# Differential attention scores from 64-row to 128-row matmuls, in a two-layer encoder

## The chip, the cores and the metric

One core of one Trainium2 chip runs the whole program. The metric is the device time of one execution in microseconds, as the median over the runs of a kernel; lower is better. A profile is taken of one further execution, and its trace tells when each instruction of each engine ran: TensorE (PE, matmuls, with its weight loads as PEld), VectorE (DVE), ScalarE (ACT), GpSimd (POOL), and SyncE (SP), which here only issues the weight transfers.

## What is computed

The reference is a trunk of two layers on 256 tokens of width 2048, all in float32. Cut to what matters here, a layer is:

```python
z = rmsnorm(x, g_mix[i]) @ w_in[i]
dq, dk, dv, cq, ckv, kr, ga, gb = jnp.split(z, split_at, axis=-1)
# differential attention: 8 heads, each with two maps of 64 columns of queries and keys
dq = apply_partial_rope(dq...); dk = apply_partial_rope(dk...)
scores = jnp.einsum('bqhcd,bkhcd->bhcqk', qb, kh) * 64 ** -0.5
probs = jax.nn.softmax(scores, axis=-1)
weights = probs[:, :, 0] - lam * probs[:, :, 1]
A = jnp.einsum('bhqk,bkhe->bqhe', weights, v)
# latent attention B: q from cq @ w_q_up, k and v from ckv @ w_kv_up, 8 heads of 128 + 64 columns
merged = sigmoid(ga) * (rmsnorm(A) @ w_branch_diff) + sigmoid(gb) * (B @ w_branch_mla)
x = x + merged @ w_out
x = x + SwiGLU(rmsnorm(x))
x = x + sigmoid(rmsnorm(x) @ w_ple_gate) * (p @ w_ple_in)
```

Head h of the differential attention has 128 columns of queries and 128 of keys; the first 64 belong to map 0 and the last 64 to map 1. Each map has its own 256x256 scores.

## The kernel before

**Layout.** Activations are held transposed: 128 features on the partitions, 256 tokens along the row. To keep float32 accuracy at the speed of the faster float32r matmul, every operand is kept as two parts: `hi` is the value rounded to float32r (an ACT copy) and `lo` is the rest (a DVE subtraction). An activation operand such as `ua[j]` is one tile of 512 columns, `hi` in the first 256 and `lo` in the last 256.

**Products.** `product` (with `piece` and `emit`) makes one 128x256 output tile: for each 128x128 weight tile one matmul with `hi` of the weight against the 512 columns (L219) and one with `lo` of the weight against the first 256 columns (L223). The weights come in pieces of eight such tiles. A piece costs one transfer on SP's queue into `w`, one ACT copy into `whi` (L194) and one DVE subtraction into `wlo` (L76). `whi` and `wlo` have three buffers each, `w` four. `joined` (L247) adds the two halves of the result: an ACT copy `join` and a DVE addition into a tile `a`.

**Differential head h.** `queries_keys(h)` makes the query product and the key product; each is joined, rotated (DVE: a stream shuffle, two multiplications, an addition, each 256 wide) and split into `hi` and `lo` by `split` (L254). Queries go to `ub[h]`, keys to `fa(h)`. `diff_weights(h)` then makes the scores: `three` (L410) names three pairs, hi x lo, lo x hi and hi x hi, for the rows 0 to 63 (map 0) and the rows 64 to 127 (map 1), and `scores` (L413) issues them for two blocks of 128 queries, the two maps alternating. These are twelve matmuls of 64 rows (L421). Both maps go through `exps` (DVE maximum, scaling, two ACT exponentials, DVE reciprocal) and are combined into `E`. `turned` transposes `E` on PE (L439) and `diff_out` multiplies with the values (L679).

**Order.** A scheduler that orders instructions by a simulated timeline writes the order of every engine's queue; each engine then takes its own queue strictly in order and waits on semaphores. The source gives it the program: `pipelined` walks over the heads, and between the steps of one head the generator `beside` supplies other work: the up-projections of the latent keys (`keys_up`, L604 on), the next head's `queries_keys`, the rotated shared key, and after the last head the latent queries and the first tiles of the gate `ga` (`gate`). Gate tiles 0 to 6 are made early into spare scratch tiles, and the first two of them go to the `sq` scratch buffers.

**Names.** In the trace `S` is a scores bank, `mm` a product bank, `at` a small bank (transposes, attention output), `E` the attention weights, `nm` the negated row maxima. The latent attention's scores come from the same `scores` function, with operands of all 128 rows (`fb` keys, `fa` queries, `kr` the rotated shared key): ten matmuls a head.

Of the kernel before, what the change touches and what calls it, by code (L numbers as in the profile page):

```python
# [12 lines left out]
F32 = mybir.dt.float32  # L13
F32R = mybir.dt.float32r
I32 = mybir.dt.int32
AF = mybir.ActivationFunctionType
ALU = mybir.AluOpType
AX = mybir.AxisListType

P = 128  # L20
T = 256
# [3 lines left out]
DH = 8  # L25
# [29 lines left out]
def encoder(ctx, tc, x, p, positions, cols, lams, wq, wk, wv, wcq, wckv, wkr, wga, wgb,  # L55
            w_q_up, w_kn, w_v, w_bd, w_bm, w_out, w_gate, w_up, w_down, w_pin, w_pg, rope_c, out):
    nc = tc.nc
    V, A, PE = nc.vector, nc.scalar, nc.tensor
# [4 lines left out]
    tmp = pool("tmp")  # L63
    stat = pool("stat")
# [4 lines left out]
    def scratch(tag, bufs, n=T):  # L69
        return tmp.tile([P, n], F32, tag=tag, name=tag, bufs=bufs)  # L70
# [4 lines left out]
    def tt(o, a, b, op):  # L75
        return V.tensor_tensor(out=o, in0=a, in1=b, op=op)  # L76

    def stt(o, a, s, b, op0, op1):
        return V.scalar_tensor_tensor(out=o, in0=a, scalar=s, in1=b, op0=op0, op1=op1)

    def ts(o, a, s1, s2, op0, op1=ALU.bypass):
        return V.tensor_scalar(out=o, in0=a, scalar1=s1, scalar2=s2, op0=op0, op1=op1)  # L82


    ua = [const.tile([P, 2 * T], F32R, name=f"ua{j}") for j in range(NC)]
# [8 lines left out]
    def operand(t):  # L94
        return t.rearrange("p c t -> p (c t)")
# [131 lines left out]
    def product(src, us, inside=None):  # L227


        acc = bank(ps_mm, "mm", "mm")  # L230
        n = len(us)
        for a in range(0, n, PT):
            m = min(PT, n - a)
            hi, lo = piece(src[:, a * P : (a + m) * P], m)
            emit(acc, hi, lo, 0, us[a : a + m], a == 0, a + m == n, inside and (inside[0] - a, inside[1]))
        return acc
# [10 lines left out]
    def joined(acc, o=None):  # L247
        t = scratch("join", 3)
        A.activation(t, acc[:, T:], AF.Copy)  # L249
        o = scratch("a", 4) if o is None else o  # L250
        tt(o, acc[:, :T], t, ALU.add)
        return o

    def split(u, src, gain=None):  # L254
        hi, lo = u[:, :T], u[:, T:]
        if gain is None:
            return A.activation(hi, src, AF.Copy), tt(lo, src, hi.bitcast(F32), ALU.subtract)  # L257
        return A.activation(hi, src, AF.Copy, scale=gain), stt(lo, src, gain, hi.bitcast(F32), ALU.mult, ALU.subtract)
# [108 lines left out]
    for t in krs:  # L367
        nc.gpsimd.memset(t.bitcast(F32), 0.0)

    def rotated(a, c_, s_, o=None):  # L370
        if o is None:
            r = bank()[:, :T]
            PE.matmul(r, halves, a, start=True, stop=True)
        else:
            r = a
        t = scratch("sh", 2)
        V.stream_shuffle(t, r, SWAP16)
        tt(t, t, s_, ALU.mult)
        tt(a, r, c_, ALU.mult)
        tt(a, a, t, ALU.add)  # L380
        if o is None:
            hi, rest = krs
            A.activation(hi[:, :T], a, AF.Copy)
            for j in range(2):
                s, t = slice(64 * j, 64 * j + 64), slice(j * T, (j + 1) * T)
                tt(rest[s, t], a[s], hi[s, :T].bitcast(F32), ALU.subtract)
        else:
            A.activation(o.rearrange("p (h t) -> p h t", h=2), a.rearrange("p (h t) -> p h t", h=1).to_broadcast([P, 2, T]), AF.Copy)
            for j in range(2):
                s, t = slice(64 * j, 64 * j + 64), slice(j * T, (j + 1) * T)  # L390
                tt(o[64 - 64 * j : 128 - 64 * j, t], a[s], o[s, t].bitcast(F32), ALU.subtract)

    def narrow(src, us):

# [15 lines left out]
    def three(q, k):  # L410
        return [(q[:, :T], k[:, T:]), (q[:, T:], k[:, :T]), (q[:, :T], k[:, :T])]

    def scores(*maps):  # L413


        Ss = [bank(ps_s, "S", "S", (P, 2, T)) for _ in maps]
        for b in range(2):
            for j in range(len(maps[0])):
                for S, pairs in reversed(list(zip(Ss, maps))):
                    q, k = pairs[j]  # L420
                    PE.matmul(S[:, b, :], q[:, b * P : (b + 1) * P], k, start=j == 0, stop=j == len(pairs) - 1)  # L421
        return Ss

    def exps(S, E, scale):

        nm, sm, rs = (stat.tile([P, 2], F32, tag=t, name=t, bufs=4) for t in ("nm", "sm", "rsum"))
        V.tensor_reduce(out=nm, in_=S, axis=AX.X, op=ALU.max, negate=True)
        ts(nm, nm, scale, None, ALU.mult)
        for b in range(2):
            last_exp[0] = A.activation(E[:, b, :], S[:, b, :], AF.Exp, bias=nm[:, b : b + 1], scale=scale, accum_out=sm[:, b : b + 1])  # L430
        V.reciprocal(out=rs, in_=sm)
        return rs
# [72 lines left out]
    for L in range(DEPTH):  # L505
# [40 lines left out]
            tt(o, t, R, ALU.mult)  # L546


        qk = [(ub[h], operand(fa(h, F32R))) for h in range(DH)]

        def queries_keys(h, *inside):
            for which, w in enumerate((wq, wk)):
                a = joined(product(w[L, h], ua, inside=(8, inside[which]) if inside else None))
                sh = scratch("sh", 2)
                V.stream_shuffle(sh, a, ROPE16)
                tt(sh, sh, sr, ALU.mult)
                tt(a, a, cr, ALU.mult)
                tt(a, a, sh, ALU.add)
                split(qk[h][which], a)


        cq, ckv = ub[8:12], ub[12:14]
# [41 lines left out]
        def beside():  # L604

            for h in range(2, DH):
                if h < 6:
                    keys_up(2 * h - 4)
                elif h == 7:
                    rotated(joined(narrow(wkr[L], ua)), crm, srm)  # L610
                yield
                queries_keys(h)
                yield
            for n in (8, 0, 2, 10):
                if n == 0:
                    settle(0)
                gate(wga, gate_a, next(todo))
                queries_up(n)
                yield
            settle(4)  # L620
            for n in (4, 6):
                gate(wga, gate_a, next(todo))
                queries_up(n)
            gate(wga, gate_a, next(todo))

        def gate(w, store, n):
            tt(store(n), joined(product(w[L, n], ua)), R, ALU.mult)
# [34 lines left out]
        def diff_weights(h):  # L662
            q, k = qk[h]
            E = [weights(), weights("E1")]
            halves = [slice(c * 64, (c + 1) * 64) for c in range(2)]
            r = [exps(S, e, 0.125) for S, e in zip(scores(*(three(q[d], k[d]) for d in halves)), E)]
            ts(r[1], r[1], neg_lam[:, L : L + 1], None, ALU.mult)
            for b in range(2):
                A.activation(E[0][:, b, :], E[0][:, b, :], AF.Copy, scale=r[0][:, b : b + 1])
                stt(E[0][:, b, :], E[1][:, b, :], r[1][:, b : b + 1], E[0][:, b, :], ALU.mult, ALU.add)  # L670
            return E[0]

        def diff_out(h, W):
# [347 lines left out]
```

## Time and profile before

| | |
|---|---|
| median of 3 runs | 2827.76 us (2827.31 to 2827.99) |
| profiled execution, its own time | 2827.12 us |
| its span, first to last instruction | 2825.3 us |
| granted TensorE clock | 0.999 |
| PE busy, PEld busy | 100%, 88% |
| DVE busy, ACT busy | 74%, 54% |
| transfers | 531 MB, mean 188 GB/s |

The differential heads run from about 106 to 211 us of the span in layer 0 and from about 1510 to 1615 us in layer 1. In the timelines the first column is the start, the second the duration. A matmul's duration there is its whole passage through the array; matmuls overlap, so what one costs is read from the distance of one start to the next.

### The profile page before, as it was taken

To read this page: it belongs to the slowest core of one execution; us is meant where nothing else is said; L and a number is where in the kernel's file an instruction comes from. 1 tells how busy PE (TensorE), PEld (TensorE's weight loads), DVE (VectorE), ACT (ScalarE), POOL (GpSimd) and SP (SyncE) were. 2 spreads that over 40 slices of the span, in tenths; PEclk is the share of its full clock that TensorE was granted. 3 is DMA by queue.
4 is the path that set the end of the run, shared out by engine and by line. 5 is a ranking of instruction groups with operands and counts; after the bars stand their busy time and mean duration, and the time that the engine had idled before them with its cause. 6 is when DMAs were issued, how large, how long until landed. Compare 5 with 4: busy or idle time off the path is not lost.

```text
span 2825.3 us, 43994 instructions
## 1 busy us (share of the span) xinstructions
PE 2816.8 (100%) x16691; PEld 2490.3 (88%) x16691; DVE 2080.3 (74%) x3573; ACT 1534.1 (54%) x2556; POOL 1.9 (0%) x15
## 2 busy tenths in 40 slices
PE   9999999999999999999999999999999999999998
PEld 8888988888888888888888889888888888888888
DVE  8998668776666666677869976687766666666777
ACT  7676546554444444455646765465544444444556
POOL 0000000000000000000000000000000000000000
PEclk9999999999999999999999999999999999999999
DMA  7545456555665566666665454555566655655654
GB/s 246 174 162 172 157 186 197 193 193 194 188 198 194 190 194 198 193 194 193 194 193 166 157 173 157 193 198 193 194 194 189 198 193 185 202 194 194 193 193 155
DMA packets 158325, 531.37 MB, mean 188 GB/s; under 512 B 17184, under 2 KB 25376, under 8 KB 158112
## 3 DMA queue, kind: packets, MB, share of 16 engines
q1 hardware_dynamic: 157680, 527.96, 58.2%
q8 instruction: 131, 2.15, 0.3%
q14 instruction: 82, 0.67, 0.1%
q10 hardware_dynamic: 432, 0.59, 0.1%
HBM read 526.39 MB, written 2.10 MB: 187 GB/s over the span
## 4 chain that ended last, share of the span: by engine, by line
PE 99%; DMA 0%; DVE 0%; SPq 0%; DVEq 0%; ACT 0%; issue 0%
PE mm L219 61%; PE mm L223 31%; PE S L421 1%; PE mmv L481 1%; PE mmv L483 1%; PE mmv L482 1%; PE at L439 1%; PE at L679 1%; PE at L735 0%; PE mm L826 0%; PE mm L407 0%; DMA w<-in_wv 0%; PE at L694 0%; PE at L332 0%; PE mm L882 0%; PE at L300 0%
## 5 line engine op out<-in xcount | busy, mean ns | idle before, releaser
L194 ACT ACTIVATE whi<-w 128x1024 fp32r<-128x1024 f32 (+2 forms) x1038 | 1065.9, 1028 | 1224.9 <-issue 593.4
L76 DVE TENSOR_TENSOR wlo<-w,whi 128x1024 fp32r<-128x1024 f32 (+2 forms) x1038 | 1225.8, 1182 | 648.0 <-ACT whi L194 642.3
L219 PE MATMUL mm<-ub,whi 128*128 128x512 f32 x3936 | 1340.5, 389 | 0.0
L219 PE MATMUL mm<-ua,whi 128*128 128x512 f32 x3712 | 1274.0, 390 | 0.0
L223 PE MATMUL mm<-ub,wlo 128*128 128x256 f32 x3936 | 1084.6, 276 | 0.0
L223 PE MATMUL mm<-ua,wlo 128*128 128x256 f32 x3712 | 1027.4, 277 | 0.0
L219 PEld LDWEIGHTS mm<-ub,whi 128*128 128x128 f32 x3936 | 737.8, 188 | 151.8
L219 PEld LDWEIGHTS mm<-ua,whi 128*128 128x128 f32 x3712 | 696.2, 188 | 141.5
L223 PEld LDWEIGHTS mm<-ub,wlo 128*128 128x128 f32 x3936 | 738.8, 188 | 1.3
L223 PEld LDWEIGHTS mm<-ua,wlo 128*128 128x128 f32 x3712 | 697.1, 188 | 2.0
L76 DVE TENSOR_TENSOR a<-mm,join 128x256 f32<-128x256 f32 (+1 forms) x423 | 174.8, 417 | 1.7 <-ACT join L855 1.4
L249 ACT ACTIVATE join<-mm 128x256 f32<-128x256 f32 x452 | 165.6, 368 | 6.3 <-PE mm L223 5.7
L76 DVE TENSOR_TENSOR xT<-xT,mm 128x256 f32<-128x256 f32 x256 | 106.9, 420 | 40.8 <-PE mm L223 37.0
L76 DVE TENSOR_TENSOR a<-a,row 128x256 f32<-128x256 f32 (+1 forms) x209 | 87.6, 422 | 5.9
L76 DVE TENSOR_TENSOR a<-a 128x256 f32<-128x256 f32 x120 | 50.9, 425 | 4.0
L76 DVE TENSOR_TENSOR ua<-a,ua 128x256 fp32r<-128x256 f32 x120 | 50.0, 418 | 1.0 <-ACT ua L257 1.0
L257 ACT ACTIVATE ua<-a 128x256 fp32r<-128x256 f32 x120 | 48.1, 403 | 2.6 <-DVE a L76 2.6
L481 PE MATMUL mmv<-whi,ua 128*128 128x512 f32 x128 | 49.0, 394 | 0.4 <-ACT whi L194 0.2
L430 ACT ACTIVATE E<-S,nm 128x256 f32<-128x256 f32 x96 | 44.2, 472 | 8.0 <-DVE nm L82 8.0
L482 PE MATMUL mmv<-whi,ua 128*128 128x512 f32 x128 | 48.4, 391 | 0.0
L483 PE MATMUL mmv<-wlo,ua 128*128 128x512 f32 x128 | 42.4, 392 | 0.0
L76 DVE TENSOR_TENSOR ssq<-ssq,sq 128x256 f32<-128x256 f32 x96 | 40.2, 419 | 0.3 <-ACT sq L287 0.3
(207 smaller groups left out, 1211.4 us busy)
## 6 DMA issues: line engine op xcount, KB each, us to landing
w<-in_w_gate SPq DMA_DIRECT2D x176, 512.0 KB, 4.6
w<-in_w_up SPq DMA_DIRECT2D x176, 512.0 KB, 4.7
w<-in_w_down SPq DMA_DIRECT2D x128, 512.0 KB, 4.2
w<-in_wga SPq DMA_DIRECT2D x64, 512.0 KB, 3.8
w<-in_wgb SPq DMA_DIRECT2D x64, 512.0 KB, 3.8
w<-in_w_out SPq DMA_DIRECT2D x64, 512.0 KB, 4.6
w<-in_w_pg SPq DMA_DIRECT2D x64, 512.0 KB, 4.6
w<-in_w_down SPq DMA_DIRECT2D x64, 384.0 KB, 3.7
```

The source lines that it names most:

```text
L76: return V.tensor_tensor(out=o, in0=a, in1=b, op=op)
L194: last_split[:] = A.activation(hi[:, s], w[:, s], AF.Copy), tt(lo[:, s], w[:, s], hi[:, s].bitcast(F32), ALU.subtract)
L219: lead = PE.matmul(acc, hi[:, s], u, start=start, stop=False)
L223: rest = PE.matmul(acc[:, T:], lo[:, s], u[:, :T], start=False, stop=stop)
L249: A.activation(t, acc[:, T:], AF.Copy)
L257: return A.activation(hi, src, AF.Copy), tt(lo, src, hi.bitcast(F32), ALU.subtract)
L421: PE.matmul(S[:, b, :], q[:, b * P : (b + 1) * P], k, start=j == 0, stop=j == len(pairs) - 1)
L430: last_exp[0] = A.activation(E[:, b, :], S[:, b, :], AF.Exp, bias=nm[:, b : b + 1], scale=scale, accum_out=sm[:, b : b + 1])
L439: PE.transpose(tp[:, kb, b * P : (b + 1) * P], W[:, b, kb * P : (kb + 1) * P], ident)
L481: PE.matmul(banks[k][b], xh, hi[:, s], start=c == 0, stop=False)
L482: PE.matmul(banks[k][b], xl, hi[:, s], start=False, stop=False)
L483: last_mm[:] = [PE.matmul(banks[k][b], xh, lo[:, s], start=False, stop=c == n - 1)]
```

## The change

The scores of a differential head are made with all 128 rows. The tile that `stacked` writes has, for map 0, the `hi` of the queries in rows 0 to 63 and their `lo` in rows 64 to 127 (first 256 columns), and for map 1 the `lo` in rows 0 to 63 and the `hi` in rows 64 to 127 (last 256 columns). The key tile of each map holds the same 64 rows of keys twice, in both row halves: a `split` on 64 rows and then an ACT copy of the 64x512 result to the other half. One matmul against the keys' `lo` and one against their `hi` then give all products of a map, so a head has two maps x two matmuls x two query blocks = eight matmuls in place of twelve. The product lo x lo, which was left out before, is now in the sum.

With it the two products of a head are joined into one tile of 2 x 256 columns (`qk`, taken from the tag `wt`), so that the shuffle and the three rotation steps run once at 512 wide instead of twice at 256. The key tiles alternate between `fa(4), fa(5)` and `fa(6), fa(7)`. In `diff_weights` the two maps' maxima, sums and reciprocals lie in one tile of four columns, which saves one scaling and one reciprocal a head. Last, in `beside` one gate tile is made before the first `keys_up`, and the one that stood at the end is gone; the number of gate tiles is the same.

```diff
--- before.py
+++ after.py
@@ -367,6 +367,12 @@
     for t in krs:
         nc.gpsimd.memset(t.bitcast(F32), 0.0)
 
+    def stacked(o, a):
+        A.activation(o.rearrange("p (h t) -> p h t", h=2), a.rearrange("p (h t) -> p h t", h=1).to_broadcast([P, 2, T]), AF.Copy)
+        for j in range(2):
+            s, t = slice(64 * j, 64 * j + 64), slice(j * T, (j + 1) * T)
+            tt(o[64 - 64 * j : 128 - 64 * j, t], a[s], o[s, t].bitcast(F32), ALU.subtract)
+
     def rotated(a, c_, s_, o=None):
         if o is None:
             r = bank()[:, :T]
@@ -385,10 +391,7 @@
                 s, t = slice(64 * j, 64 * j + 64), slice(j * T, (j + 1) * T)
                 tt(rest[s, t], a[s], hi[s, :T].bitcast(F32), ALU.subtract)
         else:
-            A.activation(o.rearrange("p (h t) -> p h t", h=2), a.rearrange("p (h t) -> p h t", h=1).to_broadcast([P, 2, T]), AF.Copy)
-            for j in range(2):
-                s, t = slice(64 * j, 64 * j + 64), slice(j * T, (j + 1) * T)
-                tt(o[64 - 64 * j : 128 - 64 * j, t], a[s], o[s, t].bitcast(F32), ALU.subtract)
+            stacked(o, a)
 
     def narrow(src, us):
 
@@ -546,17 +549,27 @@
             tt(o, t, R, ALU.mult)
 
 
-        qk = [(ub[h], operand(fa(h, F32R))) for h in range(DH)]
+        qk = {}
+
+        def two(row):
+            return row.rearrange("p (h t) -> p h t", h=1).to_broadcast([P, 2, T])
 
         def queries_keys(h, *inside):
+            a, sh = (tmp.tile([P, 2, T], F32, tag="wt", name=n, bufs=4) for n in ("qk", "qksh"))
             for which, w in enumerate((wq, wk)):
-                a = joined(product(w[L, h], ua, inside=(8, inside[which]) if inside else None))
-                sh = scratch("sh", 2)
-                V.stream_shuffle(sh, a, ROPE16)
-                tt(sh, sh, sr, ALU.mult)
-                tt(a, a, cr, ALU.mult)
-                tt(a, a, sh, ALU.add)
-                split(qk[h][which], a)
+                joined(product(w[L, h], ua, inside=(8, inside[which]) if inside else None), a[:, which, :])
+            V.stream_shuffle(operand(sh), operand(a), ROPE16)
+            tt(sh, sh, two(sr), ALU.mult)
+            tt(a, a, two(cr), ALU.mult)
+            tt(a, a, sh, ALU.add)
+            q, k = a[:, 0, :], a[:, 1, :]
+            ks = [operand(fa(j + (4 if h in (1, 3, 5) else 6), F32R)) for j in range(2)]
+            qk[h] = ub[h], ks
+            stacked(ub[h], q)
+            for j in range(2):
+                s, t = slice(64 * j, 64 * j + 64), slice(64 - 64 * j, 128 - 64 * j)
+                split(ks[j][s], k[s])
+                A.activation(ks[j][t], ks[j][s].bitcast(F32), AF.Copy)
 
 
         cq, ckv = ub[8:12], ub[12:14]
@@ -604,6 +617,8 @@
         def beside():
 
             for h in range(2, DH):
+                if h == 2:
+                    gate(wga, gate_a, next(todo))
                 if h < 6:
                     keys_up(2 * h - 4)
                 elif h == 7:
@@ -621,7 +636,6 @@
             for n in (4, 6):
                 gate(wga, gate_a, next(todo))
                 queries_up(n)
-            gate(wga, gate_a, next(todo))
 
         def gate(w, store, n):
             tt(store(n), joined(product(w[L, n], ua)), R, ALU.mult)
@@ -662,12 +676,21 @@
         def diff_weights(h):
             q, k = qk[h]
             E = [weights(), weights("E1")]
-            halves = [slice(c * 64, (c + 1) * 64) for c in range(2)]
-            r = [exps(S, e, 0.125) for S, e in zip(scores(*(three(q[d], k[d]) for d in halves)), E)]
-            ts(r[1], r[1], neg_lam[:, L : L + 1], None, ALU.mult)
+            qs = [q[:, d * T : (d + 1) * T] for d in range(2)]
+            Ss = scores(*([(a, b[:, T:]), (a, b[:, :T])] for a, b in zip(qs, k)))
+            nm, sm, r = (stat.tile([P, 4], F32, tag=t, name=t, bufs=2) for t in ("nm4", "sm4", "r4"))
+            for d, S in enumerate(Ss):
+                V.tensor_reduce(out=nm[:, 2 * d : 2 * d + 2], in_=S, axis=AX.X, op=ALU.max, negate=True)
+            ts(nm, nm, 0.125, None, ALU.mult)
+            for d, S in enumerate(Ss):
+                for b in range(2):
+                    j = 2 * d + b
+                    last_exp[0] = A.activation(E[d][:, b, :], S[:, b, :], AF.Exp, bias=nm[:, j : j + 1], scale=0.125, accum_out=sm[:, j : j + 1])
+            V.reciprocal(out=r, in_=sm)
+            ts(r[:, 2:], r[:, 2:], neg_lam[:, L : L + 1], None, ALU.mult)
             for b in range(2):
-                A.activation(E[0][:, b, :], E[0][:, b, :], AF.Copy, scale=r[0][:, b : b + 1])
-                stt(E[0][:, b, :], E[1][:, b, :], r[1][:, b : b + 1], E[0][:, b, :], ALU.mult, ALU.add)
+                A.activation(E[0][:, b, :], E[0][:, b, :], AF.Copy, scale=r[:, b : b + 1])
+                stt(E[0][:, b, :], E[1][:, b, :], r[:, 2 + b : 3 + b], E[0][:, b, :], ALU.mult, ALU.add)
             return E[0]
 
         def diff_out(h, W):
```

Three places show how the order moved. The first is PE's queue around the scores of head 1, first before, then changed (`S` is the scores bank, `fa` the keys, `ub` the queries, `at<-ident,E` the transposes).

```order
L219 MATMUL mm<-ua_84,whi 128x512
L421 MATMUL S<-fa_640,ub_93 128x256 x12
L439 MATMUL at<-ident,E 128x128 x4
L223 MATMUL mm<-ua_84,wlo 128x256
L219 MATMUL mm<-ua_85,whi 128x512
```

```order
L223 MATMUL mm<-ub_105,wlo 128x256
L442 MATMUL at<-ident,E 128x128 x4
L424 MATMUL S<-fa_1236,ub_93 128x256
L424 MATMUL S<-fa_1235,ub_93 128x256
...
L219 MATMUL mm<-ua_76,whi 128x512
L223 MATMUL mm<-ua_76,wlo 128x256
```

The run of twelve has become eight that alternate between the two key tiles (two of them are shown), they stand behind the transposes instead of ahead of them, and they stand between two products instead of inside one.

The second place is ACT's queue where the keys of head 1 become ready (before: `fa_640` are its keys, `a` its rotated product; changed: `ub_93` its queries, `fa_1235` and `fa_1236` its two key tiles).

```order
L194 ACTIVATE whi<-w_1560 128x1024
L669 ACTIVATE E<-E,rsum 128x256 x2
L257 ACTIVATE fa_640<-a 128x256
L194 ACTIVATE whi<-w_1582 128x1024
L249 ACTIVATE join<-mm 128x256 x2
```

```order
L371 ACTIVATE ub_93<-qk 128x512
L257 ACTIVATE fa_1235<-qk 64x256
L257 ACTIVATE fa_1236<-qk 64x256
L194 ACTIVATE whi<-w_1513 128x512
L249 ACTIVATE join<-mm 128x256
L257 ACTIVATE fb_1349<-a 128x256
L692 ACTIVATE E<-E,r_1261 128x256 x2
L194 ACTIVATE whi<-w_1581 128x1024
L572 ACTIVATE fa_1235<-fa_1235 64x512
L572 ACTIVATE fa_1236<-fa_1236 64x512
L194 ACTIVATE whi<-w_1603 128x1024
```

One ACT step on the keys has become four (two on 64 rows by 256, two on 64 rows by 512), and the queries' step has become one of 512 columns; they stand between the weight splits `whi` in the same queue.

The third is SP's queue of weight transfers in layer 0, behind the key weights of head 1.

```order
L191 DMA w_1180<-in_wk 128x1024
L191 DMA w_1202<-in_wk 128x1024
L191 DMA w_1290<-in_w_kn 128x2x256
L191 DMA w_1365<-in_wq 128x1024
L191 DMA w_1387<-in_wq 128x1024
```

```order
L191 DMA w_1167<-in_wk 128x1024
L191 DMA w_1189<-in_wk 128x1024
L191 DMA w_1277<-in_wga 128x1024
L191 DMA w_1299<-in_wga 128x1024
L191 DMA w_1326<-in_w_kn 128x2x256
L191 DMA w_1394<-in_wq 128x1024
```

The two transfers of the early gate tile have moved ahead of the first latent-key weights, and everything behind them comes two transfers later.

## The prediction, made before the change was run

> **What bounds the kernel now.** I read the page first, its busy line and its chain of waits.
>
> ```profile
> PE 2816.8 (100%) x16691; PEld 2490.3 (88%) x16691; DVE 2080.3 (74%) x3573; ACT 1534.1 (54%) x2556; POOL 1.9 (0%) x15
> PE 99%; DMA 0%; DVE 0%; SPq 0%; DVEq 0%; ACT 0%; issue 0%
> ```
>
> TensorE works without a break, and 99% of the chain that ends last is PE. So two things alone can move the time: what a matmul costs on PE, and a new wait that stops PE. No wait is there to be removed. A busy PE hides its own inefficiency, though, so I went on to the timeline of PE. Around the scores of head 1 it reads:
>
> ```profile
> 123.31 0.39 PE L219 MATMUL mm<-ua,whi 128*128 128x512 f32 x1
> 123.54 0.28 PE L223 MATMUL mm<-ua,wlo 128*128 128x256 f32 x1
> 123.65 0.39 PE L219 MATMUL mm<-ua,whi 128*128 128x512 f32 x1
> 123.88 0.28 PE L223 MATMUL mm<-ua,wlo 128*128 128x256 f32 x1
> 123.99 0.39 PE L219 MATMUL mm<-ua,whi 128*128 128x512 f32 x1
> 124.31 0.98 PE L421 MATMUL S<-fa,ub 64*128 64x256 f32 x12
> 125.22 0.66 PE L439 MATMUL at<-ident,E 128*128 128x128 f32 x4
> 125.63 0.36 PE L223 MATMUL mm<-ua,wlo 128*128 128x256 f32 x1
> 125.83 0.40 PE L219 MATMUL mm<-ua,whi 128*128 128x512 f32 x1
> 126.06 0.28 PE L223 MATMUL mm<-ua,wlo 128*128 128x256 f32 x1
> 126.18 0.39 PE L219 MATMUL mm<-ua,whi 128*128 128x512 f32 x1
> ```
>
> From start to start an undisturbed L219 matmul costs 0.23 us (123.31 to 123.54) and an L223 matmul 0.11 us. The twelve scores take 0.91 us from their first start to the next work (124.31 to 125.22). That is 0.076 us each, less than an undisturbed matmul of the same 256 columns, so two 64-row matmuls run side by side. But the L219 matmul ahead of them takes 0.32 us instead of 0.23: PE loses 0.09 us on entering the block. At head 0, where products follow directly, the edges show on both sides:
>
> ```profile
> 106.48 0.28 PE L223 MATMUL mm<-ub,wlo 128*128 128x256 f32 x1
> 106.68 0.97 PE L421 MATMUL S<-fa,ub 64*128 64x256 f32 x12
> 107.58 0.50 PE L219 MATMUL mm<-ub,whi 128*128 128x512 f32 x1
> 107.92 0.28 PE L223 MATMUL mm<-ub,wlo 128*128 128x256 f32 x1
> ```
>
> Entering costs 0.20 - 0.11 = 0.09 us, the twelve 0.90 us, and the first matmul behind them 0.34 instead of 0.23 us, 0.11 more. A block of half-row scores thus takes 1.10 us of PE. Scores with all 128 rows are in the trace too, in the latent attention:
>
> ```profile
> 309.52 0.28 PE L223 MATMUL mm<-ua,wlo 128*128 128x256 f32 x1
> 309.64 0.52 PE L421 MATMUL S<-fb,fa 128*128 128x256 f32 x3
> 310.00 0.40 PE L421 MATMUL S<-kr,fc 128*128 128x256 f32 x2
> 310.24 0.52 PE L421 MATMUL S<-fb,fa 128*128 128x256 f32 x3
> 310.60 0.40 PE L421 MATMUL S<-kr,fc 128*128 128x256 f32 x2
> 310.83 0.60 PE L439 MATMUL at<-ident,E 128*128 128x128 f32 x4
> 311.19 0.48 PE L219 MATMUL mm<-ua,whi 128*128 128x512 f32 x1
> 311.50 0.28 PE L223 MATMUL mm<-ua,wlo 128*128 128x256 f32 x1
> ```
>
> Ten of them take 1.19 us (309.64 to 310.83), 0.119 us each, and the matmul ahead of them takes 0.12 us, 0.01 more than undisturbed. The four transposes take 0.36 us and leave the next product 0.08 us late (0.31 for 0.23). In the block of head 1 transposes follow as well and take 0.41 us with the product behind them 0.09 us late (0.20 for 0.11), so there only 0.05 us of that belongs to the half-row scores: its block costs 0.09 + 0.91 + 0.05 = 1.05 us.
>
> **The change on PE.** Removed: twelve half-row matmuls a head, 1.05 to 1.10 us; I take 1.08. Added: eight full-row matmuls, 8 x 0.119 = 0.95 us, plus 0.01 at the entry, 0.96. What a product directly behind a full-row block loses is not in these rows: nothing at best, the 0.11 us of head 0 at worst. I take nothing, since the entry shows none and the whole array is in use on both sides. So a head gains 0.12 us, and 16 heads (8 in each of two layers) gain 1.9 us. Bounds: at worst 1.05 - 0.96 - 0.11 = -0.02 us a head, a loss of 0.3 us in all; at best 1.10 - 8 x 0.11 = 0.22 us (full-row matmuls as fast as an undisturbed L223), 3.5 us in all. The gate tile moves 16 pairs of matmuls, 16 x 0.34 = 5.4 us of PE, and its two transfers from one place to another, and adds none.
>
> **The change on DVE and ACT.** They are off the chain, so their terms are nothing as long as PE has its operands in time. How far from the limit they are is shown by the stretch of the differential heads (columns of the last row: PE, PEld, DVE and ACT busy, with counts) and by the groups in it:
>
> ```profile
> core 0: us, PE busy (x) PEld busy (x) DVE busy (x) ACT busy (x) POOL busy (x), PEclk, DMA share, GB/s
> 111.50:222.90 111.40, 111.40 (x718) 97.67 (x717) 106.26 (x270) 84.55 (x215) 0.00 (x0) 1.00 0.49 160
> L76 DVE TENSOR_TENSOR a<-mm,join 128x256 f32<-128x256 f32 x34 | 13.8, 417 | 0.1
> L76 DVE TENSOR_TENSOR fa<-a,fa 128x256 fp32r<-128x256 f32 x11 | 4.6, 421 | 0.2 <-ACT fa L257 0.2
> L76 DVE TENSOR_TENSOR wlo<-w,whi 128x512 fp32r<-128x512 f32 x3 | 2.0, 682 | 0.0
> L555 DVE STREAM_SHUFFLE sh<-a 128x256 f32<-128x256 f32 x13 | 5.8, 445 | 0.0
> L76 DVE TENSOR_TENSOR ub<-a,ub 64x256 fp32r<-64x256 f32 x4 | 1.7, 420 | 0.1
> L431 DVE RECIPROCAL rsum<-sm 128x2 f32<-128x2 f32 x16 | 2.5, 158 | 0.5 <-ACT E L430 0.2
> L82 DVE TENSOR_SCALAR nm<-nm 128x2 f32<-128x2 f32 x16 | 2.1, 160 | 0.0
> L249 ACT ACTIVATE join<-mm 128x256 f32<-128x256 f32 x34 | 12.5, 377 | 1.4 <-PE mm L223 1.1
> L194 ACT ACTIVATE whi<-w 128x1024 fp32r<-128x1024 f32 x38 | 40.4, 1064 | 21.0 <-PE mm L219 17.8 <-issue 1.4 <-ACT join L249 1.0
> L257 ACT ACTIVATE fa<-a 128x256 fp32r<-128x256 f32 x11 | 4.6, 422 | 0.9 <-DVE a L76 0.9
> L388 ACT ACTIVATE ub<-a 128x512 fp32r<-128x512 f32 x2 | 1.3, 644 | 0.0
> ```
>
> DVE, a head: the two shuffles and six rotation steps (2 x 0.445 + 6 x 0.42 = 3.41 us) become four steps of 512 columns. A shuffle of 512 is not in the trace; I price it like the 512-wide subtraction, 0.68 (below by one 256-wide shuffle, 0.445, above by two, 0.89), so 4 x 0.68 = 2.72. Two subtractions become four on 64 rows, which cost no less than on 128 (0.420 against 0.421): +0.84. One scaling and one reciprocal go: -0.32. The sum is -0.17 us a head (-0.41 to +0.04): DVE stays at its 95%. ACT, a head: two splits of 0.42 become one of 512 columns (0.64), two on 64 rows (0.42 each) and two copies of 64x512 (0.64 each, on the same grounds): 2.76 for 0.84, +1.9 us. Some seven heads in the stretch add 13 us to ACT's 84.55 of 111.4, and it has 26.9 us idle there. So there is room, but ACT's idle time falls by half, and the added steps stand in the same queue as the `whi` splits, each waiting for DVE: behind them wait the next `whi`, then DVE's `wlo`, then PE.
>
> The longer way from the key product to the scores is the second danger. Before: join 0.38, addition 0.42, shuffle 0.445, three steps 1.26, split 0.42 and 0.42, 3.3 us. After: 0.38 + 0.42 + four steps of 0.68 + the queries' split 0.64 + key split 0.42 and 0.42 + two copies 1.28 = 6.3 us, 3.0 more. The smallest margin that I found before is at head 7, where the last key operand is written here and the scores start there:
>
> ```profile
> 203.09 0.42 DVE L76 TENSOR_TENSOR fa<-a,fa 128x256 fp32r<-128x256 f32 x1
> 206.69 0.97 PE L421 MATMUL S<-fa,ub 64*128 64x256 f32 x12
> ```
>
> 206.69 - 203.51 = 3.2 us, just over the 3.0. The new order also puts more PE work between a head's key product and its scores: counted out in both orders at 0.34 us a pair, 10.3 us became 22.2 at head 7 and 12.1 became 14.7 at head 0; only head 2 loses (18.3 to 16.3), head 3 keeps 16. So I cost the waits at nothing. The gate tile is part of this: 5.4 us of PE work that asks DVE for two `wlo` and two small steps, where the heads ask it for more.
>
> **The sum.** The profiled execution took 2827.12 us, 1.8 us around its span of 2825.3. Less 1.9 it comes to 2825.2. The median of the runs is 0.64 us higher than that execution, so the forecast for the median is 2827.76 - 1.9 = **2825.9 us**, 0.07% faster. I count 0.2%, 5.7 us, as what a measurement of this kernel tells from no change; the forecast lies inside.
>
> **Rivals.** *The edges stay.* Half-row matmuls run in pairs, so twelve need six slots and the change needs eight; if the 0.09 and 0.11 us at the edges come from changing between products and scores, and not from the half rows, they remain. Then a head pays 8 x 0.119 - 0.905 = +0.05 us, 0.8 us in all: 2828.5, not faster, within 0.2%. Against it stands the latent block, whose entry costs 0.01. The Trainium skill's page TensorEngine Tiling (Array Packing), under Overview (Theoretical Speedup) and Tiling Modes (Key Properties), speaks against the change: tiles of half the rows run independently, up to twice as fast; by that alone six slots of 0.119 become eight, 16 x 0.24 = +3.8 us, 2831.6. The same list says that a change of tiling mode drains TensorE; the 0.09 us at the entry and 0.11 behind agree with that, and the 0.90 us for six pairs, 0.15 a pair, is not the full doubling either.
>
> *Scores come late (slower).* If each of the three added ACT steps stands behind one `whi` split of 1.06 us, the way grows by 3.0 + 3.2 = 6.2 us against a margin of 3.2. At the heads whose cover does not grow PE then waits: head 3 3.0 us, head 2 5.0, 8.0 a layer, 16 in all, less 1.9: 2841.9, 0.5% slower. It decides from the point where the way has grown by more than margin and added cover. For it: DVE at 95% and both engines strictly in order. Against it: the 26.9 us that ACT has idle, and a PE order with 14.7 us or more behind every key product.
>
> *Fewer matmuls, plainly.* 64 fewer at the 0.28 us of a row is 18 us: 2809.9, 0.6% faster. Against it: a duration is a passage through the array, and all sixteen old blocks together cost 16 x 1.08 = 17 us.
>
> **Chances.** Forecast 0.77, edges stay 0.12, scores late 0.07, plain count 0.02, something else 0.02. The likeliest is the time I predict. Its own range from the bounds is 2824.3 (all of the 3.5 us) to 2828.1 (a loss of 0.3). The 8 in 10 takes in the edges that stay and small waits, half a microsecond more than those 2828.5: 2829.0; downward I add 0.5 us for pairs that run at 0.35 us behind a half-row block (125.83 to 126.18) instead of 0.34 (123.31 to 123.65): 2823.8. Faster by over 0.2% (under 2822.1) 0.02; slower by over 0.2% (above 2833.4), most of the late scores, 0.05; within 0.93.
>
> **What would show it.** In the profile after, eight scores in 0.95 us with the matmul ahead at its undisturbed distance show the first term; 0.2 us still lost at the edges shows the first rival. A PE that stays in the chain for 99%, with no wait for DVE or ACT at the scores or at L223 around 110 to 215 us, shows the second. ACT's busy time should rise by 16 x 1.9 = 30 us and DVE's fall slightly. The prediction is wrong if PE stands idle for more than 2 us in a layer, or if full-row blocks slow the pairs behind them.

## The result, and the profile after

| | before | after |
|---|---|---|
| median of 9 runs each | 2827.35 us (2826.82 to 2827.99) | 2835.35 us (2834.55 to 2836.84) |
| ratio, 95% interval | | 1.0029 (1.0020 to 1.0038) |
| span of the profiled execution | 2825.3 us | 2833.5 us |

The changed kernel is 8.0 us slower, 0.29%. The forecast was 2825.9 us with a range up to 2829.0: the sign was wrong, and the time lies outside the range. The busy line and the chain of the changed kernel's page, and below them PE's own waits in its trace (total, times, longest):

```profile
PE 2817.6 (99%) x16627; PEld 2496.0 (88%) x16627; DVE 2087.9 (74%) x3493; ACT 1564.1 (55%) x2604; POOL 1.9 (0%) x15
PE 97%; ACT 2%; DVE 0%; issue 0%; DMA 0%; DVEq 0%; SPq 0%; ACTq 0%
PE mm L219 <- DVE qk L76: 5.9, 6, 1.6
PE at L500 <- DVE ones L116: 1.0, 1, 1.0
PE at L717 <- DVE ub L79: 0.8, 2, 0.4
PE mm L219 <- DVE a L76: 0.5, 2, 0.2
PE mmv L484 <- ACT whi L194: 0.4, 1, 0.4
```

PE's own waits in the kernel before were these, and the only one of this size is the 1.0 us for `ones` at the start:

```profile
PE at L497 <- DVE ones L116: 1.0, 1, 1.0
PE mmv L481 <- ACT whi L194: 0.2, 1, 0.2
```

PE now waits 7.2 us more in the heads and behind them, 5.9 of it in six waits for one kind of instruction: the DVE addition that joins a product into `qk`. PE's busy time rose by 0.8 us, although it was to fall by 1.9. So the span's 8.2 us are waits, about 7.4 (with 0.2 more at `mmv`), and 0.8 us of busy time. That is not work that was added: there are 64 matmuls fewer, but the first one behind a wait shows 0.47 us where 0.39 is usual. The stretch of the differential heads in layer 0 shows the same (columns as in the prediction):

```profile
111.50:222.90 111.40, 108.32 (x663) 96.37 (x662) 101.75 (x213) 90.91 (x213) 0.00 (x0) 1.00 0.49 159
```

PE stands for 3.1 of 111.4 us, more than the 2 us a layer that the prediction named as the sign of being wrong, and DVE, the supposed tight engine, is less busy than before (101.75 against 106.26). Nothing is overloaded. Something is out of place.

**Where PE stands.** PE's timeline after the scores of head 1:

```profile
126.63 0.60 PE L442 MATMUL at<-ident,E 128*128 128x128 f32 x4
127.38 1.21 PE L424 MATMUL S<-fa,ub 128*128 128x256 f32 x8
130.15 0.47 PE L219 MATMUL mm<-ua,whi 128*128 128x512 f32 x1 [1.56 <-DVE qk L76]
...
145.73 0.47 PE L219 MATMUL mm<-ua,whi 128*128 128x512 f32 x1 [0.69 <-DVE qk L76]
...
161.22 0.47 PE L219 MATMUL mm<-ua,whi 128*128 128x512 f32 x1 [0.69 <-DVE qk L76]
```

Behind the scores of heads 1, 2 and 3 the first matmul of a query product waits, and the same three waits come again about 1407.6 us later in layer 1. The product does not read `qk`. By the names in the built order it writes a product bank: the product banks (`mm`) are four, given out in turn, and the query product that starts at 130.15 (head 3's) gets the bank of the query product of head 2, which is free only when DVE has added its two halves. When ACT and DVE did that, their timelines tell:

```profile
123.60 0.36 ACT L249 ACTIVATE join<-mm 128x256 f32<-128x256 f32 x1
...
124.97 1.04 ACT L194 ACTIVATE whi<-w 128x1024 fp32r<-128x1024 f32 x1
126.04 1.28 ACT L572 ACTIVATE fa<-fa 64x512 fp32r<-64x512 f32 x2
127.35 1.06 ACT L194 ACTIVATE whi<-w 128x1024 fp32r<-128x1024 f32 x1
```

```profile
128.44 1.22 DVE L76 TENSOR_TENSOR wlo<-w,whi 128x1024 fp32r<-128x1024 f32 x1 [1.17 <-ACT whi L194]
129.58 0.75 DVE L76 TENSOR_TENSOR qk<-mm,join 128x256 f32<-128x256 f32 x2
```

ACT had its half of the query's join ready at 123.96. The addition comes at 129.58, 5.6 us later and side by side with the key's (x2). It is not late because DVE has no time: DVE stands idle for 1.17 us ahead of the step in front of it. It is late because it was written behind that step, a `wlo` split, in DVE's queue, whose `whi` came late because ACT made the two key copies between its splits. The chain of waits in the window from 126 to 131 us names these links (start, length, what):

```profile
126.69 0.63 ACT fa L572
...
127.35 1.07 ACT whi L194
...
128.44 0.58 DVE wlo L76
129.02 0.56 issue
129.58 0.43 DVE qk L76
130.01 0.14 issue
130.15 0.47 PE mm L219
```

**What else the trace shows.** An undisturbed block, at head 4:

```profile
176.38 0.39 PE L219 MATMUL mm<-ua,whi 128*128 128x512 f32 x1
176.61 1.12 PE L424 MATMUL S<-fa,ub 128*128 128x256 f32 x8
177.57 0.28 PE L223 MATMUL mm<-ua,wlo 128*128 128x256 f32 x1
```

Eight scores take 0.96 us, and the matmul ahead keeps its 0.23 us: the first term stands as forecast. By the distances from start to start and their usual values, the blocks of heads 1 to 3 cost 3.18, 1.89 and 1.91 us in place of 0.97, which is 4.1 us of excess a layer; another 0.6 us a layer is lost later, at 232 us, where the transposes of the attention output in `settle` wait 0.4 us and the product behind them 0.2.

### The profile page after: what moved, and what is told of

Read it like the earlier page. It is cut to its first block, busy times and chain, and to the rows that moved or that the text cites. A ratio compares the mean times of both kernels' runs of the same rounds, so it can differ in the third digit from the quotient of the medians.

```text
span 2833.5 us, 43839 instructions
## 1 busy us (share of the span) xinstructions
PE 2817.6 (99%) x16627; PEld 2496.0 (88%) x16627; DVE 2087.9 (74%) x3493; ACT 1564.1 (55%) x2604; POOL 1.9 (0%) x15
## 4 chain that ended last, share of the span: by engine, by line
PE 97%; ACT 2%; DVE 0%; issue 0%; DMA 0%; DVEq 0%; SPq 0%; ACTq 0%
PE mm L219 60%; PE mm L223 30%; PE mmv L486 1%; PE mmv L484 1%; PE mmv L485 1%; PE S L424 1%; ACT whi L194 1%; PE at L702 1%; PE at L758 0%; PE at L442 0%; PE mm L849 0%; ACT E L688 0%; PE mm L410 0%; ACT fa L572 0%; DVE wlo L76 0%
## 5 line engine op out<-in xcount | busy, mean ns | idle before, releaser
L76 DVE TENSOR_TENSOR a<-mm,join 128x256 f32<-128x256 f32 x391 | 161.9, 417 | 1.5 <-ACT join L878 1.4
L76 DVE TENSOR_TENSOR a<-a,sig 128x256 f32<-128x256 f32 x92 | 38.4, 419 | 0.0
```

## The experiments

Three theories were to be told apart. **A, the join's place:** the merged tile `qk` and its shuffled partner take their buffers from the tag `wt` (a tag names a set of buffers, here four, that its tiles share), which also serves the transposed weights, and this holds the query's join back in DVE's queue, so that a product bank comes free late. **B, the load:** the key copies and the longer way to the scores take too much of ACT and DVE, so that operands come late whatever the buffers. **C, the gate tile:** putting it early does harm. All medians stand beside the kernel before on the same chip, which took 2827.2 to 2827.3 us in each comparison.

**1. Own buffers for the merged tile.** From the changed kernel, with four buffers in all as it had, only split by use (the second part of the latent attention's transposed weights moves to the new two as well):

```diff
-        wt = [tmp.tile([P, 2, T], F32R if parts else F32, tag="wt", name="wt", bufs=4) for _ in range(1 + parts)]
+        wt = [tmp.tile([P, 2, T], F32R if parts else F32, tag=("wt", "qs")[j], name="wt", bufs=2) for j in range(1 + parts)]
...
-            a, sh = (tmp.tile([P, 2, T], F32, tag="wt", name=n, bufs=4) for n in ("qk", "qksh"))
+            a, sh = (tmp.tile([P, 2, T], F32, tag="qs", name=n, bufs=2) for n in ("qk", "qksh"))
```

> The changed kernel, with the joined query-key tile and its shuffled copy in two buffers of their own instead of sharing four with the transposed weights (the transposed weights get two, and the latent attention's second part uses the new two). Theory A (the shared buffers hold the query product's join back in VectorE's queue until the transposed weights of an earlier head have a buffer, so its accumulator bank is freed late and TensorE waits for a bank): the waits behind the scores of heads 1 to 3 go (4.1 us a layer), and so does most of the rest; the gain on the half-row scores stays: 2825 to 2827 us, 8 to 10 us under the change as given. Theory B (the key copies load ScalarE, weight splits and scores come late): the copies are all still there, so 2833 us or more.

Measured: 2826.88 us, ratio 0.9998 (0.9990 to 1.0007); 8.5 us less than the changed kernel. ACT's join of the same product, and DVE's addition:

```profile
123.05 0.37 ACT L249 ACTIVATE join<-mm 128x256 f32<-128x256 f32 x1
```

```profile
124.33 0.42 DVE L76 TENSOR_TENSOR qk<-mm,join 128x256 f32<-128x256 f32 x1
```

The addition now follows the copy after 0.9 us, and the waits for `qk` are gone; what is left of PE's waits is the start:

```profile
PE at L500 <- DVE ones L116: 1.1, 1, 1.1
PE mmv L484 <- ACT whi L194: 0.2, 1, 0.2
```

The sum of work on DVE and ACT is the same (2087.5 and 1564.8 us busy), so the load alone does not make the 8.5 us: A is the main cause. The number of buffers did not change either, only who shares them.

**2. Not merged at all.** Queries and keys are joined and rotated apart, 256 wide, in the scratch tiles of before; stacked scores, key copies, four-column statistics and the early gate tile stay:

```diff
-            a, sh = (tmp.tile([P, 2, T], F32, tag="wt", name=n, bufs=4) for n in ("qk", "qksh"))
             for which, w in enumerate((wq, wk)):
-                joined(product(w[L, h], ua, inside=(8, inside[which]) if inside else None), a[:, which, :])
-            V.stream_shuffle(operand(sh), operand(a), ROPE16)
...
+                a = joined(product(w[L, h], ua, inside=(8, inside[which]) if inside else None))
+                sh = scratch("sh", 2)
+                V.stream_shuffle(sh, a, ROPE16)
+                tt(sh, sh, sr, ALU.mult)
+                tt(a, a, cr, ALU.mult)
+                tt(a, a, sh, ALU.add)
+                if not which:
+                    stacked(ub[h], a)
```

> The changed kernel, but query and key product are again joined and rotated each by itself at 256 wide, in the tiles they had before; the eight full-row score matmuls, the stacked queries, the ScalarE key copies and the gate tile's place stay. Theory A: the late joins are gone, 2825 to 2828 us. Theory B: copies as in the change, 2833 us or more.

Measured: 2825.51 us (2824.88 to 2825.79), ratio 0.9994 (0.9985 to 1.0003). Its busy line and the heads' stretch:

```profile
PE 2814.9 (100%) x16627; PEld 2492.8 (88%) x16627; DVE 2091.7 (74%) x3573; ACT 1563.6 (55%) x2604; POOL 1.9 (0%) x15
111.50:222.90 111.40, 111.40 (x690) 99.61 (x689) 107.85 (x255) 95.17 (x220) 0.00 (x0) 1.00 0.49 165
```

Here PE's busy time is 1.9 us below the 2816.8 of before, the sum that the prediction had for the stacked scores, and PE does not stand once in the heads although DVE and ACT do more than in the changed kernel (107.85 and 95.17 us of 111.4). It is the fastest version found. Its interval takes in 1, so a gain of 0.06% is not secured, though none of its 11 runs reaches down into the range of the kernel before (2826.66 to 2828.22).

**3. The merge alone.** The kernel before, with queries and keys joined into one tile of the tag `wt` and rotated 512 wide; half-row scores, no copies, gate tile late:

```diff
+            a, sh = (tmp.tile([P, 2, T], F32, tag="wt", name=n, bufs=4) for n in ("qk", "qksh"))
             for which, w in enumerate((wq, wk)):
-                a = joined(product(w[L, h], ua, inside=(8, inside[which]) if inside else None))
...
+                joined(product(w[L, h], ua, inside=(8, inside[which]) if inside else None), a[:, which, :])
+            V.stream_shuffle(operand(sh), operand(a), ROPE16)
...
+            for which in range(2):
+                split(qk[h][which], a[:, which, :])
```

> The kernel before, with one part of the change alone: query and key products joined into one tile from the buffers of the transposed weights and rotated at 512 wide. Scores, splits and the gate tile stay as before, and there are no key copies. Theory A: TensorE waits for accumulator banks at several heads, 5 to 12 us slower than the kernel before (2832 to 2839 us). Theory B: nothing is slower, since ScalarE does no more than before: 2826 to 2828 us.

Measured: 2830.03 us, ratio 1.0010 (1.0002 to 1.0019), 2.8 us over before, which is between the ranges of A and B. PE waits in the heads also without copies and stacked scores, though less:

```profile
PE mm L219 <- DVE a L76: 1.4, 2, 0.7
...
PE S L421 <- DVE fa L76: 0.5, 2, 0.2
```

The query's additions are held back here as well, by 4.7 to 10.8 us behind their copies from head 2 on, but PE waits for none of them: its waits are for another addition (`a`) and for keys (`fa`). So the shared buffers hold the joins back by themselves, which costs 1.7 us against the same merge in own buffers in experiment 8, and 8.5 us where the rest of the change stands in the queues too.

**4. The gate tile late.** The changed kernel, with the one gate tile back behind the latent queries:

```diff
             for h in range(2, DH):
-                if h == 2:
-                    gate(wga, gate_a, next(todo))
                 if h < 6:
...
                 queries_up(n)
+            gate(wga, gate_a, next(todo))
```

> The changed kernel with the gate tile back at its old place, behind the last latent queries. Theory A: the shared buffers are still there and TensorE has 5.4 us less of other work ahead of the first heads, so the waits stay or grow: 2834 to 2842 us. Theory B: the same or slower. Theory C (the moved gate tile itself does the harm, by taking TensorE time and transfers ahead of the first latent keys): back to 2825 to 2828 us.

Measured: 2841.65 us, ratio 1.0052 (1.0039 to 1.0065), 6.3 us more than the changed kernel. C falls: the early gate tile helps. The waits without it:

```profile
PE mm L219 <- DVE qk L76: 3.4, 2, 1.8
PE at L442 <- DVE E L79: 3.3, 2, 1.7
PE mm L219 <- DVE a L76: 3.2, 3, 1.5
```

Not all of the 6.3 us is waiting. PE's waits add up to 11.6 us here and to 8.6 in the changed kernel, 3.0 more. The rest is the clock. PE waits 1.65 us ahead of the transposes at 123.15 us and 1.50 us behind them, and the matmuls that follow were granted about half of TensorE's clock (0.53, the third number from the end; columns as above):

```profile
125.50:129.00 3.50, 3.41 (x11) 2.93 (x12) 3.50 (x9) 1.92 (x5) 0.00 (x0) 0.53 0.56 176
```

A pair of product matmuls, one with `whi` and one with `wlo`, costs 0.64 us there and 0.35 behind that stretch. Layer 1 has the same two waits and the same slow pairs. I estimate the loss from this row at 3.5 x 0.47 = 1.6 us a layer, 3.3 in both. In the changed kernel the clock stayed at 1.00 around its wait of 1.56 us, and no other run here has such a stretch in its heads; from how long a wait the clock falls is not shown.

**5. and 6. The gate tile late, without the shared buffers.** The same edit on the versions of 2 and of 1.

> The kernel before with the stacked queries, the key copies, the eight full-row matmuls and the four-column statistics alone: no joined query-key tile, and the gate tile at its old place. Theory A (shared buffers held the join back, and only that made the change slow): nothing holds the joins back, so the gain of 1.9 us on the scores shows with or without the gate tile, 2825 to 2827 us. Theory B' (the copies and the longer way to the scores do need cover, which the early gate tile gives): 1 to 6 us slower than with the gate tile ahead, 2827 to 2832 us.

> The changed kernel with buffers of their own for the joined tile, and the gate tile at its old place. Theory A: of the 6.3 us that the gate tile was worth with shared buffers most goes with the waits for banks, so 2826 to 2829 us. Theory B': the copies and the 512-wide steps need the cover, 2829 to 2834 us.

Measured: 2828.61 us, ratio 1.0005 (0.9996 to 1.0014), and 2831.08 us, 1.0013 (1.0004 to 1.0022). Without the gate tile these rise by 3.1 and 4.2 us, into the ranges of B' and out of those of A. In the unmerged version the waits that come back are these:

```profile
PE mm L223 <- DVE wlo L76: 1.4, 4, 0.4
```

In the version with own buffers they are 1.6 us for `a`, 0.7 for `qk` and, at the scores, 0.5 for the key copies. There B has its part: with the copies and the longer way in the queues weight splits, additions and keys come late for PE, unless 5.4 us of gate work a layer stands in between. Where that work is there, nothing of it shows among PE's waits, though with own buffers some scores start late (see the account below).

**7. and 8. The other two edits alone.** The kernel before with the gate tile early and nothing else (the edit of 4 the other way round); and the kernel before with the merge of 3 in own buffers (the tags of 1).

> The kernel before with the gate tile moved ahead of the first latent keys and nothing else. Both theories: TensorE was never without work there, so no change, 2826.5 to 2828 us; VectorE is nearly full in this stretch and gets some room, which cannot show in the time.

> The kernel before with query and key products joined into one tile and rotated at 512 wide, as in the run of that part alone, but with two buffers of their own for the joined tile and its shuffled copy. Theory A: the 2.8 us that the joined tile cost with shared buffers go away, 2826.5 to 2828 us. If the 512-wide steps themselves were at fault: 2829.5 to 2831 us.

Measured: 2829.04 us, ratio 1.0006 (0.9997 to 1.0015), and 2828.36 us, 1.0004 (0.9995 to 1.0013). Both intervals take in 1, and both medians lie above the expected 2826.5 to 2828, by 1.0 and 0.4 us. The one wait of PE that grew in the first is at `mmv`, from 0.2 to 0.8 us. It is at 6.5 us of the span, ahead of all that was edited; the rest of its 1.7 us over before I can't place. The merge in own buffers shows no wait in the heads.

**9. and 10. The key copies off ACT.** The chain above holds key copies between two weight splits, so the changed kernel and the version of 2 were run with the copies on GpSimd:

```diff
-                A.activation(ks[j][t], ks[j][s].bitcast(F32), AF.Copy)
+                nc.gpsimd.tensor_copy(out=ks[j][t], in_=ks[j][s].bitcast(F32))
```

> The changed kernel with its two key copies a head made by GpSimd instead of ScalarE; all else as changed, the shared buffers too. The chain that ends at the stalled product of head 1 holds 1.0 us of the key copies in ACT's queue, between two weight splits. If the place of the query's addition in DVE's queue alone makes the wait, and ACT's load only has room to spare, the time stays at 2834 to 2837 us. If the copies lengthen that chain, the second weight split starts 1.3 us earlier (126.04 instead of 127.35), the waits of 1.56 and twice 0.69 us a layer shrink by 1.3 and up to 0.69 each, 2 x 2.7 = 5.4 us in all: 2830 us (2829 to 2832). The price of a GpSimd copy of 64 x 512 is in no trace here; if two of them take over 4 us a head, the scores come late and the time rises over 2837.

> The version that joins and rotates queries and keys apart, with the key copies on GpSimd. TensorE waited nowhere in the heads of that version, so taking 1.3 us a head off ACT can give nothing: 2825.5 us, within 1.0, whichever theory holds. Over 2828 if the GpSimd copies make the scores late.

Measured: 2833.22 us, ratio 1.0022 (1.0013 to 1.0031), and 2829.54 us, 1.0008 (0.9999 to 1.0017). Both miss. The changed kernel falls by 2.1 us only, a little under the 2834 to 2837 of "place alone" and above the 2829 to 2832 of "the copies lengthen the chain"; the other version loses 4.0 us where nothing was expected. PE's waits changed in kind: in the changed kernel the six for `qk` are gone, and it waits 2.7 us for other additions (`a`), 1.1 for `wlo` and 1.0 for `E`; the other version waits six times for `wlo`, 2.0 us in all. The groups of the heads' stretch, first the version of 2, then the same with copies on GpSimd:

```profile
L76 DVE TENSOR_TENSOR fb<-a,fb 128x256 fp32r<-128x256 f32 x8 | 3.4, 421 | 0.0
L82 DVE TENSOR_SCALAR nm<-nm 128x4 f32<-128x4 f32 x7 | 1.1, 164 | 0.0
```

```profile
L76 DVE TENSOR_TENSOR fb<-a,fb 128x256 fp32r<-128x256 f32 x8 | 4.0, 506 | 0.1
L82 DVE TENSOR_SCALAR nm<-nm 128x4 f32<-128x4 f32 x7 | 1.9, 265 | 0.1
```

The same DVE steps got longer (421 to 506 ns, 164 to 265), and the scheduler wrote another order, since the copies had left ACT's queue. So the runs took away one load and brought two other changes, and they do not size the copies' share in the changed kernel. They show that GpSimd is no free place for them, and that with 17.5 us less on ACT (1546.6 busy in place of 1564.1) the changed kernel is still 6 us slower than before.

## Why the prediction was wrong, point by point

**The stacked scores: right.** The full-row block was put at 0.96 us and takes 0.96; in the version of experiment 2 PE's busy time fell by 1.9 us, the forecast sum. That it agrees to the tenth is partly luck, since busy time differs by as much between the kernel before (2816.8 us) and the merge in own buffers (2818.7), which have the same matmuls. The blocks carry the claim: all sixteen of experiment 2 take 0.95 us, or 1.02 to 1.04 directly behind transposes, and a product matmul behind them takes its usual time. The rival that the edges stay falls with it, and so does what the Trainium skill's page TensorEngine Tiling (Array Packing) would give by the doubling of half-row tiles alone, the 2831.6 us of the prediction.

**ACT: right, DVE: wrong, and without weight.** ACT's busy time rose by 30.0 us (1534.1 to 1564.1), as forecast. DVE's rose by 7.6 us where a fall of 2.7 (16 x 0.17) was forecast. The 512-wide rotation steps measure 693 ns and the shuffle 747, where I had 680 for all, which is 0.1 us a head. Part of the rest is that neighbours on DVE overlap (two additions of 0.42 take 0.75 together), so that fewer and wider steps save less than their durations say; I have not split it further. The version of experiment 2 has more DVE work in the heads' stretch than the changed kernel, 107.85 us against 101.75, and is the fastest, so this term did not decide.

**The step that failed: "So I cost the waits at nothing".** It stood on a margin measured at the scores, from the last key operand to the first score, and on the PE work counted between a head's key product and its scores. At the scores that was nearly right: in head 1 the last key copy ends at 127.32 and the scores start at 127.38, 0.4 us later than the transposes ahead of them would let them (126.63 + 0.36). The larger wait was one that I had not looked for. Joining the queries and keys in one tile put a new user on the tag `wt`, and a product's bank is not free before its join. I priced the merged steps by their durations, and did not ask where the join would stand in DVE's queue, nor how long the product bank would be held. The traces have the answer: from head 2 on, the query's addition starts 5.6 to 10.6 us behind the end of its copy, where it was 0.4 to 1.4 us before. At head 2 of the kernel before the two steps are:

```profile
115.79 0.38 ACT L249 ACTIVATE join<-mm 128x256 f32<-128x256 f32 x1
```

```profile
116.86 0.42 DVE L76 TENSOR_TENSOR a<-mm,join 128x256 f32<-128x256 f32 x1
```

With own buffers it is 0.8 to 1.5 us at heads 2 to 5 and 5.2 and 2.4 us at heads 6 and 7, and 8.5 us are back. A late addition is not a wait by itself: at heads 5 to 7 of the change it is 7.3 to 10.6 us late, and no product waited for it.

Why the scheduler wrote the addition there shows in the built orders, that is, in the lists of the instructions of all engines as it placed them. The program asks for the transposed weights of head 0 (`wt`, written by `turned`) ahead of the merged tile of head 2, and so on from head to head. With the shared tag the query's addition, the first write into the merged tile, stands directly behind ACT's first write into that `wt` tile, at all six heads from head 2 on and in both layers, in the changed kernel as in experiment 3. The buffer that it writes had its last use before, so no buffer was lacking; it was held by the order in which the tag hands its buffers out. With own buffers the addition stands ahead of that write. ACT's copy at head 2 in the traces, first of the change, then with own buffers:

```profile
129.79 0.60 ACT L444 ACTIVATE wt<-at 128x512 f32<-128x512 f32 x1
```

```profile
129.51 0.61 ACT L444 ACTIVATE wt<-at 128x512 f32<-128x512 f32 x1
```

The addition starts at 129.58 and at 124.33. Over the two layers of the change the two steps start within 0.3 us of each other at each of these heads; with own buffers the addition is 5.2 to 9.5 us ahead. That the sharing makes the loss is shown by experiment 1, which changes nothing but who shares the buffers.

**The rival "scores come late": the right sign, a neighbouring mechanism.** It asked for added ACT steps behind `whi` splits, and the key copies between two splits are in the chain of the wait. But what PE waited for was a bank and not the scores' operands, and heads 1, 2 and 3 paid 2.2, 0.9 and 0.9 us rather than heads 2 and 3 paying 5.0 and 3.0. A chance of 0.05 for slower was too little: "DVE at 95% and both engines strictly in order" was a reason to follow each moved instruction that frees something.

**The gate tile: right that it is cover.** It is worth 6.3 us in the changed kernel (3.0 of waits and, by the estimate above, 3.3 of clock), 4.2 with own buffers and 3.1 without the merge. That it works only as cover shows in the kernel before, where PE has no waits to cover: alone it gained nothing.

**The account**, in medians from before to after: 2827.3; with the shared merge 2830.0 (+2.8); with stacked scores, copies and four-column statistics 2841.65 (+11.6, in which PE's 1.9 us are already gained and about 3.3 are lost to the clock); with the gate tile early 2835.35 (-6.3). From there own buffers give 2826.88 (-8.5), and leaving the merge out 2825.51 (-1.4). The last step fits the scores: with own buffers but merged, the blocks of heads 1 and 2 cost 1.18 and 1.32 us in place of 0.97, since the key copies end at 126.79 and the scores start at 126.84. That is 0.55 us a layer, 1.1 in all.

## What to carry to other kernels

When a change gives a temporary another owner, ask of every accumulator bank who frees it, where that instruction stands in its engine's queue, and what it shares buffers with: the duration of a step says nothing of what it holds. Count the distance in the printed order from a product's end to the instruction that empties its bank, as one counts the distance to its reader. And separate the edits: here the stacked scores gained their 1.9 us on TensorE, and the buffers of a merged tile beside them lost 8.5.

## What was not expected of the hardware

**DVE steps stand while GpSimd copies.** In experiment 10, GpSimd's timeline, and DVE's at the same time:

```profile
121.70 1.61 POOL L572 CAST fa<-fa 64x512 fp32r<-64x512 f32 x2 [14.63 <-DVE fa L76]
```

```profile
122.12 1.47 DVE L76 TENSOR_TENSOR fb<-a,fb 128x256 fp32r<-128x256 f32 x2
```

Two steps of 421 ns take 1.47 us there, where two neighbours that also read two tensors from SBUF take 0.85 (`ub<-qk,ub` at 122.34 us of the changed kernel). At another place the copy pays instead: one at 141.02 us takes 1.67 us where the one at 139.80 takes 0.68, and the `wlo` beside it keeps its 1.23. The Trainium skill's page Advanced Engine Details and Errata (GPSIMD Details) says that GpSimd shares a read and a write interface with DVE and conflicts with DVE instructions that read two tensors from SBUF; these do, and the trace agrees. No addition `a<-mm,join`, which reads one operand from the product bank, ran beside a copy in this trace, so it shows nothing of them. The scaling `nm` reads one tensor and got longer too (0.47 and 0.58 us beside a copy); the page names a mode that uses both ports as the other case, and no run here shows whether `nm` ran in it.

**Four product banks in turn are not enough by being four.** The Trainium skill's page Perfetto Trace Analysis (Optimizing Tensor Performance, Matmuls) advises to rotate matmul groups through different banks, so that emptying one overlaps the next group. Both kernels do so. The trace agrees as long as the emptying keeps its place: with the addition 0.9 us behind its copy PE never stood, and with it 5.6 us behind PE waited 1.56 us, though not every late addition made a wait. No run here tried another number of banks.
